# Macaron mLSTM block: early results loaded one group ahead, and a 6 + 2 split of the PSUM banks

## The chip, the core and the metric

The kernel runs on one core of a Trainium2 chip. The metric is the device time of one execution in microseconds (us), as the median of several runs. Engines are named as in the profile: PE (TensorE matmul), PEld (its weight load), DVE (VectorE), ACT (ScalarE), POOL (GpSimd) and SP (SyncE, which here only issues DMAs).

## What is computed

One layer of an encoder on a 1024 x 1024 float32 sequence: a half-step SwiGLU feed-forward (width 2816), a mixing layer (mLSTM and a gating branch), a second half-step feed-forward and a final norm. The change touches only the two feed-forwards and the end:

```
x = x + 0.5 * swiglu(rmsnorm(x, ffn1_norm_g), ffn1_w_in, ffn1_w_out)
...  # mixing layer
x = x + 0.5 * swiglu(rmsnorm(x, ffn2_norm_g), ffn2_w_in, ffn2_w_out)
return rmsnorm(x, final_norm_g)

def swiglu(x, w_in, w_out):
    gate, up = jnp.split(x @ w_in, 2, axis=-1)
    return (jax.nn.silu(gate) * up) @ w_out
```

## The kernel before

Tokens are held transposed, as tiles of 128 features by 512 tokens, in two halves of the sequence (t = 0 and 1). Each matrix is split into a rounded part and a remainder, so one product of four 128-row slices is 12 matmuls of 128 x 512 (three per slice). The feed-forwards use a fast 2 x 2 matrix scheme that needs fewer products: some of them are formed early.

`Ffn.first_products` walks over the 22 groups f of 128 hidden features and forms the products that need only the first half of the tokens. The two results of a group are an accumulated product and the SiLU of it; both are written to DRAM (`self.eb[f][0]` and `self.eb[f][1]`, "eb") through the POOL queue.

`Ffn.run` then walks over the same 22 groups, in blocks of 4, 4, 4, 4, 2 and 4. `Ffn.group(f)` loads the group's weights with four DMAs into two tiles of the pool "raw" (4 buffers; line 284), loads the two early results from DRAM into two tiles "c" (lines 329 and 331), copies the first of them into a PSUM bank x on ACT (line 333), and forms five products onto x, a copy y of it (line 338) and a third bank b (copied out on line 343). Before a product, ACT rounds the weights (line 290) and DVE takes the remainder (line 291) into a tile "fw" (4 buffers); POOL forms sums of the weights ahead of that (lines 303 to 305 and 348). The first product of a group accumulates onto x, so it can't start before the copy of line 333, and that copy can't run before its DMA has landed.

After the first group of every block but the first, the down projection of the block before runs: `down_fast` for blocks of the scheme (four steps of two weight loads, line 386, and seven products; DVE or ACT copies four results per step out into "c" tiles and POOL adds them to DRAM with an accumulating DMA, lines 409 to 424) and `down` for the block of two (16 results, lines 436 and 437). `last` does the final block's down projection: per half t and 128 output features d a product on PE (line 444), the residual add on DVE (line 471) and then the function `final`.

All "c" tiles (early results, copied products, down results) share one pool "t512" of 11 buffers. The PSUM banks, 8 in all, are split into a pool "mm" of 7 and a pool "ml" of 1 during the feed-forwards; `bank("mm")` takes from the one and `psm()` from the other.

In the second feed-forward `final` is `fin2`: it squares and accumulates xt for the norm, transposes xt with PE into a bank (line 1021; up to four 128 x 128 transposes), and DVE multiplies the bank by the norm's weights into the output tile (line 1024). After d = 7 the statistics are finished and the rows are scaled and stored. The second half of the tokens is done in two parts of 256 columns.

What sets the order: the instructions of each engine stand in a queue of their own, which runs strictly in order. The queues are fixed when the kernel is built, by a list scheduler that follows the program text as far as operands are ready, and that hands out the buffers of one pool in the order in which the text asks for them. So a tile can't be written by any instruction ahead of the first write of the tile that the text took from the same pool before it. SP's queue holds the weight loads and the loads of the early results; a weight load waits there until its raw buffer is free, and whatever stands behind it waits too.

Of the kernel before, what the change touches and what calls it, by code (L numbers as in the profile page):

```python
# [19 lines left out]
NF = DFF // P  # L20
# [14 lines left out]
def block_body(ctx, tc, x, ffn1_norm_g, ffn1_w_in, ffn1_w_out, mix_norm_g, w_mix_in, mlstm_conv_w,  # L35
               mlstm_conv_b, mlstm_b_igate, mlstm_b_fgate, mlstm_head_norm_g, sgu_norm_g, sgu_norm_b,
               sgu_w_s, sgu_b_s, w_mix_out, ffn2_norm_g, ffn2_w_in, ffn2_w_out, final_norm_g, out):
    nc = tc.nc
    V, A, PE, G = nc.vector, nc.scalar, nc.tensor, nc.gpsimd
    x = x[0]  # L40
    out = out[0]
# [8 lines left out]
    def open_psum(stack, n, **bufs):  # L50
        for tag, b in bufs.items():
            psum[tag] = stack.enter_context(
                tc.tile_pool(name=f"{tag}{n}", bufs=b, space=bass.MemoryType.PSUM, reuse_waits="tile"))

    def bank(tag):
        return psum[tag].tile([P, NH], F32, tag=tag, name=tag)

    f1 = ExitStack()
# [3 lines left out]
    def open_temps(stack, n, bufs):  # L62
        raws.append(stack.enter_context(tc.tile_pool(name=f"rawp{n}", bufs=3 if n == 2 else 4, reuse_waits="tile")))
        tps.append(stack.enter_context(tc.tile_pool(name=f"tp{n}", bufs=bufs, reuse_waits="tile")))

    open_temps(f1, 1, TMP)
    open_psum(f1, 1, mm=7, ml=1)

    def t512():
        return tps[-1].tile([P, NH], F32, tag="t512", name="t512")  # L70
# [1 line left out]
    def psm():  # L72
        return bank("ml")
# [42 lines left out]
    def pc(nm, i):  # L116
        return par[:, col[nm] + i:col[nm] + i + 1]
# [29 lines left out]
    def spread():  # L147
        if todo:
            todo.pop(0)()
# [115 lines left out]
    def evens(src):  # L265
        return src[:, :, 0, :], src[:, :, 1, :]

    class Ffn:
# [39 lines left out]
        def first_products(self, fs):  # L308
# [9 lines left out]
            for f, a, e in st:  # L318
# [2 lines left out]
                A.activation(out=e[:, 1, :], in_=a, func=AF.Silu)  # L321
                G.dma_start(out=self.eb[f][1], in_=e[:, 1, :])

        def group(self, f):
            r1, r2 = self.raw(f, 0, True), self.raw(f, 1, True)
            a11, a21 = evens(r1)
            a12, a22 = evens(r2)
            p1 = self.c512()
            nc.sync.dma_start(out=p1, in_=self.eb[f][0])
            sg1 = self.c512()  # L330
            nc.sync.dma_start(out=sg1, in_=self.eb[f][1])
            x = bank("mm")
            A.copy(out=x, in_=p1)  # L333
            s1 = self.sums(G, a11, a12, a21, a22, 4)
            w = self.unit(a11)
            self.prod(x, w, self.B["t2"], False, True)
            y = bank("mm")
            A.copy(out=y, in_=x)
            w = self.unit(s1)
            b = bank("mm")  # L340
            self.prod(b, w, self.B["t1"], True, True)
            p5 = self.c512()
            A.copy(out=p5, in_=b)
            w = self.unit(a21)
            self.prod(y, w, self.B["t3"], False, True)
            c22 = self.c512()
            V.tensor_tensor(out=c22, in0=y, in1=p5, op=ALU.add)
            G.tensor_tensor(out=a12, in0=a12, in1=a11, op=ALU.subtract)
            w = self.unit(a12)
            self.prod(x, w, self.B["22"], False, True)  # L350
            V.tensor_tensor(out=p5, in0=x, in1=p5, op=ALU.add)
            A.activation(out=p5, in_=p5, func=AF.Silu)
            w = self.unit(a22)
            self.prod(y, w, self.B["t4"], False, True)
            V.scalar_tensor_tensor(out=sg1, in0=y, scalar=0.5, in1=sg1, op0=ALU.mult, op1=ALU.mult)  # L355
            V.scalar_tensor_tensor(out=c22, in0=c22, scalar=0.5, in1=p5, op0=ALU.mult, op1=ALU.mult)
            u3 = sg1
            if f >= FAST:
                self.hs.append((self.part(self.hp, u3), self.part(bigp, c22)))
            elif f % 2 == 0:  # L360
                self.H["11"].append(self.part(self.hp, u3))
                self.odd = u3, c22
            else:
                h11, h12 = self.odd
                H = self.H
                H["21"].append(self.part(self.hp, u3))
                V.tensor_tensor(out=h11, in0=h12, in1=h11, op=ALU.subtract)
                H["t1"].append(self.part(bigp, h11))
                V.tensor_tensor(out=h12, in0=c22, in1=h12, op=ALU.subtract)
                H["t3"].append(self.part(bigp, h12))  # L370
                V.tensor_tensor(out=h11, in0=c22, in1=h11, op=ALU.subtract)
                H["t2"].append(self.part(bigp, h11))
                V.tensor_tensor(out=u3, in0=u3, in1=h11, op=ALU.subtract)
                H["22"].append(self.part(self.hp, c22))
                H["t4"].append(self.part(bigp, u3))
# [99 lines left out]

        def run(self, src, final, parts, hook):
            pend = None
            for bi, (f0, n) in enumerate(BLOCKS):
                hs = self.hs = []
                H = self.H = {k: [] for k in ("11", "21", "22", "t1", "t2", "t3", "t4")}  # L480
                for f in range(f0, f0 + n):
                    self.group(f)
                    if pend is not None:
                        pend()
                        pend = None
                    spread()
                if f0 < FAST:
                    pend = lambda f0=f0, H=H: self.down_fast(f0, H, src)
                elif bi < len(BLOCKS) - 1:
                    pend = lambda f0=f0, n=n, hs=hs: self.down(f0, n, hs, src)  # L490
                else:
                    self.last(f0, n, hs, src, final, parts, hook)
# [488 lines left out]
        xn2, bcs, st = mix(mx, xnm)  # L981

    with ExitStack() as f2:
        open_psum(f2, 3, mm=7, ml=1)
        open_temps(f2, 3, TMP)
        ffn2 = Ffn(f2, "2", ffn2_w_in[0], ffn2_w_out[0])
        ffn2.B["11"], ffn2.B["21"] = xn2[:4], xn2[4:]

        def get2(j, i, t):
            b = ffn2.c512()  # L990
            d = 4 * j + i
            if t == 0:
                G.dma_start(out=b, in_=xs_[1][d])
                return b
            G.dma_start(out=b, in_=xd[1][t][d])
            V.scalar_tensor_tensor(out=b, in0=b, scalar=pc("g2", d), in1=bcs[t], op0=ALU.mult, op1=ALU.mult)
            return b

        ffn2.first_products((0, 1))
        bcs.append(st.bcast())  # L1000
        for i in range(4):
            ffn2.first_products((2 * i + 2, 2 * i + 3))
            ffn2.operands(i, get2)
        for f in range(10, NF, 2):
            ffn2.first_products((f, f + 1))

        PARTS = (1, 2)
        sts = [[Stats(4 // p) for _ in range(p)] for p in PARTS]
        fgs = []
        ys = []  # L1010

        def fin2(h, d, part, xt):
            n = 4 // PARTS[h]
            if not fgs:
                fgs.append(bigp.tile([P, D], F32, tag="big", name="fg"))
                nc.sync.dma_start(out=fgs[0], in_=final_norm_g.partition_broadcast(P))
            fg = fgs[0]
            sts[h][part].add(xt)
            ps = bank("mm")
            for t in range(n):  # L1020
                PE.transpose(out=ps[:, t * P:(t + 1) * P], in_=xt[:, t * P:(t + 1) * P], identity=ident)  # L1021
            if d % 2 == 0:
                ys.append(bigp.tile([P, n, 2 * P], F32, tag="big", name="y"))
            V.tensor_tensor(out=ys[-1][:, :, (d % 2) * P:(d % 2 + 1) * P],  # L1024
                            in0=ps[:, 0:n * P].rearrange("p (t c) -> p t c", c=P),
                            in1=fg[:, None, d * P:(d + 1) * P].to_broadcast([P, n, P]), op=ALU.mult)
            if d < KT - 1:
                return
            r = sts[h][part].rstd()
            t0 = h * NH + part * n * P  # L1030
            ov = out[t0:t0 + n * P, :].rearrange("(t p) c -> p t c", p=P)
            for i in range(4):
                y = ys.pop(0)
                for t in range(n):
                    if t == n - 1:
                        A.activation(out=y[:, t, :], in_=y[:, t, :], func=AF.Copy, scale=r[:, t:t + 1])  # L1036
                    else:
                        V.tensor_scalar(out=y[:, t, :], in0=y[:, t, :], scalar1=r[:, t:t + 1], scalar2=None,  # L1038
                                        op0=ALU.mult)
                nc.sync.dma_start(out=ov[:, :, i * 2 * P:(i + 1) * 2 * P], in_=y)  # L1040

        ffn2.run(xd[1], fin2, PARTS, lambda t, xs: None)


# [25 lines left out]
```

## Time and profile before

| | before |
|---|---|
| median of 3 runs | 2380.12 us |
| lowest, highest | 2379.06, 2381.86 us |
| the profiled execution, its own time | 2376.19 us |
| its span (first to last instruction) | 2374.4 us |
| mean granted TensorE clock | 0.979 |
| PE busy | 2258.1 us (95% of the span) |
| DVE, ACT, POOL busy | 61%, 47%, 21% |

The first feed-forward's `run` goes from about 143 to 700 us, the mixing layer to about 1640, the second feed-forward's `run` from about 1755 us to the end, of which the last 85 us are `last` with `fin2`. A wait in the profile is the idle time of an engine ahead of an instruction, put down to what released it. The clock is a share of full speed (1.0 is 2.4 GHz, 0.5 is 1.2 GHz).

### The profile page before, as it was taken

How to read it: one execution, taken by the hardware profiler on the slowest of the kernel's cores; microseconds unless marked ns; L12 is line 12 of the kernel's file. 1: busy time of each engine (PE TensorE's matmuls, PEld its weight loads, DVE VectorE, ACT ScalarE, POOL GpSimd, SP SyncE). 2: the span in 40 equal slices, each digit the busy share in tenths (PEclk: the TensorE clock that was granted, in tenths of full speed). 3: DMA queues.
4: the chain of work that ended last, by engine and by line, in shares of the span. 5: the costliest groups of instructions: out<-in, count | busy, mean ns of one | idle time of the engine just before them, and what ended most of it. 6: DMA issues, size and time to landing. Idle time of an engine off the chain costs nothing. (4 is left out here: it accounts for less than half of the span.)

```text
span 2374.4 us, 30679 instructions
## 1 busy us (share of the span) xinstructions
PE 2258.1 (95%) x10979; PEld 1881.8 (79%) x10979; DVE 1453.2 (61%) x2563; ACT 1120.8 (47%) x1924; POOL 496.7 (21%) x557
## 2 busy tenths in 40 slices
PE   7999999999899999999999999999999999999896
PEld 5888787777778988888889878887887787777675
DVE  6647676675366757656656666564647576765355
ACT  5545454444444356444445455453545454544432
POOL 3242433414520000000000000001241524324420
PEclk8999999999999999999999999999999999999999
DMA  8853655637753334233343433325762745646632
GB/s 271 252 179 98 142 117 132 133 89 138 155 186 109 88 85 135 83 89 89 115 129 93 134 113 93 92 83 178 247 190 89 151 108 132 129 120 133 147 110 89
DMA packets 331512, 311.51 MB, mean 131 GB/s; under 512 B 19160, under 2 KB 279896, under 8 KB 331360
## 3 DMA queue, kind: packets, MB, share of 16 engines
q1 hardware_dynamic: 292608, 217.20, 31.1%
q0 software_dynamic: 38752, 92.36, 17.8%
q8 instruction: 86, 1.41, 0.2%
q14 instruction: 66, 0.54, 0.1%
HBM read 223.48 MB, written 86.02 MB: 130 GB/s over the span
## 5 line engine op out<-in xcount | busy, mean ns | idle before, releaser
L297 PE MATMUL mm<-b,fw 128*128 128x512 f32 x2640 | 626.4, 399 | 56.7 <-ACT mm L333 55.7
L297 PEld LDWEIGHTS mm<-b,fw 128*128 128x128 f32 x2640 | 508.1, 193 | 174.6 <-ACT mm L333 64.0
L291 DVE TENSOR_TENSOR fw<-raw,fw 128x512 fp32r<-128x512 f32 (+1 forms) x472 | 316.0, 676 | 396.4 <-ACT fw L290 394.9
L162 PE MATMUL mm<-xn,w 128*128 128x512 f32 x2304 | 546.6, 391 | 0.0
L162 PEld LDWEIGHTS mm<-xn,w 128*128 128x128 f32 x2304 | 427.0, 188 | 82.8
L297 PE MATMUL mm<-h,fw 128*128 128x512 f32 x1344 | 313.6, 393 | 5.8 <-ACT fw L290 3.1
L297 PEld LDWEIGHTS mm<-h,fw 128*128 128x128 f32 x1344 | 248.5, 188 | 69.6 <-ACT fw L290 8.2
L290 ACT CAST fw<-raw 128x512 fp32r<-128x512 f32 (+1 forms) x472 | 247.8, 526 | 101.5 <-PE mm L297 71.6
L138 DVE TENSOR_TENSOR w<-raw,w 128x1024 fp32r<-128x1024 f32 (+3 forms) x160 | 178.6, 1117 | 163.6 <-ACT w L137 163.2
L297 PE MATMUL mm<-xn,fw 128*128 128x512 f32 x1056 | 247.4, 396 | 3.6 <-ACT xn L195 2.1
L297 PEld LDWEIGHTS mm<-xn,fw 128*128 128x128 f32 x1056 | 200.5, 191 | 49.4 <-ACT xn L195 3.7
L137 ACT CAST w<-raw 128x1024 fp32r<-128x1024 f32 (+3 forms) x160 | 153.8, 963 | 178.7 <-PE mm L162 86.2
L176 PE MATMUL mm<-w,xn 128*128 128x256 f32 x1344 | 163.9, 282 | 0.0
L176 PEld LDWEIGHTS mm<-w,xn 128*128 128x128 f32 x1344 | 161.8, 189 | 1.4 <-issue 0.5
L256 POOL DMA_DIRECT2D xs<-t x16 | 8.6, 541 | 642.0 <-DVE t L253 641.3
L195 ACT CAST h<-c 128x512 fp32r<-128x512 f32 x136 | 82.2, 621 | 69.1 <-DVE c L355 26.3
L303 POOL TENSOR_TENSOR s<-raw 128x512 f32<-128x512 f32 x44 | 59.4, 1351 | 205.7 <-DMA raw<-in_ffn_w_in_dram 190.3
L444 PE MATMUL mm<-h,wl 128*128 128x512 f32 (+1 forms) x480 | 97.3, 356 | 0.3 <-DVE h L196 0.2
L196 DVE TENSOR_TENSOR h<-c,h 128x512 fp32r<-128x512 f32 x136 | 91.1, 689 | 5.9 <-ACT h L195 4.8
L409 POOL DMA_DIRECT2D xd<-c x32 | 28.0, 874 | 309.6 <-ACT fw L290 273.0
L444 PEld LDWEIGHTS mm<-h,wl 128*128 128x128 f32 x480 | 78.4, 192 | 12.5 <-DVE h L196 0.7
L162 PE MATMUL po<-mh,w 128*128 128x512 f32 x384 | 87.5, 389 | 0.0
(258 smaller groups left out, 2607.6 us busy)
## 6 DMA issues: line engine op xcount, KB each, us to landing
raw<-in_ffn_w_in_dram SPq DMA_DIRECT2D x264, 256.0 KB, 3.4
raw<-in_w_mix_in_dram SPq DMA_DIRECT2D x96, 512.0 KB, 3.8
xd<-c POOLq DMA_DIRECT2D x160, 256.0 KB, 5.2
eb<-early POOLq DMA_DIRECT2D x88, 256.0 KB, 2.8
c<-eb SPq DMA_DIRECT2D x88, 256.0 KB, 4.3
raw<-in_ffn_w_out_dram SPq DMA_DIRECT2D x72, 256.0 KB, 3.0
raw<-in_w_mix_in_dram SPq DMA_DIRECT2D x32, 384.0 KB, 3.4
xl<-xd POOLq DMA_DIRECT2D x32, 256.0 KB, 4.4
```

The source lines that it names most:

```text
L137: A.copy(out=w[:, 0, 0:n, :], in_=raw[:, 0:n, :])
L138: V.tensor_tensor(out=w[:, 1, 0:n, :], in0=raw[:, 0:n, :], in1=w[:, 0, 0:n, :].bitcast(F32), op=ALU.subtract)
L162: PE.matmul(out=banks[j], lhsT=w[:, a, i, j * P:(j + 1) * P], rhs=act[k][:, b, ts], start=(k == first and pi == 0), stop=(k == last and pi ...
L176: PE.matmul(out=o, lhsT=act[k][:, b, t * P:(t + 1) * P], rhs=w[:, a, i, :], start=(t % 2 == 0 and k == 0 and pi == 0), stop=(t % 2 == 1 an ...
L195: A.copy(out=dst[:, 0, :], in_=src)
L196: V.tensor_tensor(out=dst[:, 1, :], in0=src, in1=dst[:, 0, :].bitcast(F32), op=ALU.subtract)
L290: A.copy(out=w[:, 0], in_=src)
L291: V.tensor_tensor(out=w[:, 1], in0=src, in1=w[:, 0].bitcast(F32), op=ALU.subtract)
L297: PE.matmul(out=bank, lhsT=w[:, x, i, :], rhs=t[:, y, :], start=(start and i == 0 and pi == 0), stop=(stop and i == len(b) - 1 and pi == 2 ...
L303: G.tensor_tensor(out=s1, in0=a21, in1=a22, op=ALU.add)
L409: G.dma_start(out=acc[0][d], in_=c11, accum_op=ALU.add)
L444: PE.matmul(out=o, lhsT=w[:, x, i, :], rhs=hs[i][:, y, ts], start=(i == 0 and pi == 0), stop=(i == n - 1 and pi == 2))
```

## The change

`fetch(f)` takes two tiles from "t512" and issues the loads of the early results of group f on SP. `run` calls it once for group 0; `group(f)` uses the pair that was fetched, and fetches the pair of group f + 1 right after its own weight loads, so in the text ahead of the down projection and of the next group's weights. In both feed-forwards the banks are split 6 + 2 instead of 7 + 1, and the transposes of `fin2` take their bank from the pool of two.

```
-    open_psum(f1, 1, mm=7, ml=1)
+    open_psum(f1, 1, mm=6, ml=2)
...
+        def fetch(self, f):
+            self.ahead = self.c512(), self.c512()
+            for t, src in zip(self.ahead, self.eb[f]):
+                nc.sync.dma_start(out=t, in_=src)
+
         def group(self, f):
             r1, r2 = self.raw(f, 0, True), self.raw(f, 1, True)
             a11, a21 = evens(r1)
             a12, a22 = evens(r2)
-            p1 = self.c512()
-            nc.sync.dma_start(out=p1, in_=self.eb[f][0])
-            sg1 = self.c512()
-            nc.sync.dma_start(out=sg1, in_=self.eb[f][1])
+            p1, sg1 = self.ahead
+            if f + 1 < NF:
+                self.fetch(f + 1)
             x = bank("mm")
             A.copy(out=x, in_=p1)
...
         def run(self, src, final, parts, hook):
             pend = None
+            self.fetch(0)
...
-        open_psum(f2, 3, mm=7, ml=1)
+        open_psum(f2, 3, mm=6, ml=2)
...
             sts[h][part].add(xt)
-            ps = bank("mm")
+            ps = psm()
             for t in range(n):
```

## Rows read from the trace of the kernel before

**Rows 1.** Waits, whole span: who waited for whom, total us, times, longest us.
```profile
ACT mm L333 <- DMA c<-eb: 115.3, 40, 7.8
...
PE mm L297 <- ACT mm L333: 55.7, 18, 9.6
...
PE mm L1021 <- DVE xl L471: 16.8, 23, 3.2
...
SPq L284 <- DVE fw L291: 788.7, 163, 15.5
```
**Rows 2.** Timeline of SP's queue: start, us, operation (weights L284, early results L329).
```profile
257.99 0.44 SPq L329 DMA_DIRECT2D c<-eb  x1
...
261.24 11.91 SPq L284 DMA_DIRECT2D raw<-in_ffn_w_in_dram  x4
273.26 0.45 SPq L329 DMA_DIRECT2D c<-eb  x1
```
**Rows 3.** Timeline of PE, same stretch; in brackets idle before and its releaser.
```profile
265.03 20.93 PE L297 MATMUL mm<-b,fw 128*128 128x512 f32 x84 [3.88 <-ACT mm L333]
...
295.74 14.57 PE L297 MATMUL mm<-b,fw 128*128 128x512 f32 x63 [1.07 <-ACT mm L333]
```
**Rows 4.** Timeline of ACT, same stretch.
```profile
257.43 0.62 ACT L290 CAST fw<-raw 128x512 fp32r<-128x512 f32 x1
...
261.67 0.62 ACT L290 CAST fw<-raw 128x512 fp32r<-128x512 f32 x1
264.39 0.59 ACT L333 COPY mm<-c 128x512 f32<-128x512 f32 x1 [2.09 <-DMA c<-eb]
269.54 0.57 ACT L338 COPY mm<-mm 128x512 f32<-128x512 f32 x1 [4.57 <-PE mm L297]
```
**Rows 5.** Stretches of 8 us, PE: busy (matmuls), granted clock, DMA share, GB/s.
```profile
265.03:273.03 8.00, 8.00 (x28) 0.79 0.65 143
...
2243.99:2251.99 8.00, 8.00 (x24) 0.66 0.59 101
```
**Rows 6.** The same of a stretch behind no long wait, all engines.
```profile
273.03:281.03 8.00, 8.00 (x37) 6.61 (x36) 5.23 (x6) 3.34 (x6) 4.18 (x3) 1.00 0.39 124
```
**Rows 7.** DMA issues: count, size, median us from issue to landing.
```profile
xd<-c POOLq DMA_DIRECT2D x160, 256.0 KB, 5.2
...
c<-eb SPq DMA_DIRECT2D x88, 256.0 KB, 4.3
```
**Rows 8.** Timeline of POOL in the down projection of a two-group block.
```profile
614.60 5.06 POOL L437 DMA_DIRECT2D xd<-c  x5
626.45 1.25 POOL L303 TENSOR_TENSOR s<-raw 128x512 f32<-128x512 f32 x1 [6.78 <-DMA raw<-in_ffn_w_in_dram]
627.65 0.87 POOL L437 DMA_DIRECT2D xd<-c  x1
```
**Rows 9.** Timeline of PE at the end, steps of 512 columns.
```profile
2296.14 0.66 PE L1021 MATMUL mm<-ident,xl 128*128 128x128 f32 x4 [0.78 <-DVE xl L471]
2296.56 2.99 PE L444 MATMUL mm<-h,wl 128*128 128x512 f32 x12
2300.33 0.66 PE L1021 MATMUL mm<-ident,xl 128*128 128x128 f32 x4 [0.79 <-DVE xl L471]
```
**Rows 10.** Timeline of PE at the end, steps of 256 columns.
```profile
2331.62 0.69 PE L1021 MATMUL mm<-ident,xl 128*128 128x128 f32 x2 [3.17 <-DVE xl L471]
...
2335.39 0.44 PE L1021 MATMUL mm<-ident,xl 128*128 128x128 f32 x2 [0.52 <-DVE xl L471]
...
2337.77 0.44 PE L1021 MATMUL mm<-ident,xl 128*128 128x128 f32 x2 [0.52 <-DVE xl L471]
```
**Rows 11.** Three stretches of the end: us, PE, PEld, DVE, ACT, POOL busy (instructions), clock, DMA.
```profile
2289.69:2322.00 32.31, 25.80 (x122) 19.19 (x123) 14.68 (x23) 5.04 (x8) 3.19 (x6) 1.00 0.16 49
2326.58:2335.39 8.81, 5.12 (x29) 4.62 (x29) 6.01 (x23) 2.54 (x6) 0.00 (x0) 0.81 0.64 213
2335.39:2364.75 29.36, 23.00 (x173) 20.48 (x173) 15.68 (x45) 6.81 (x17) 0.00 (x0) 1.00 0.13 44
```

## The prediction
> **What bounds the kernel now.** I read the list of waits first, then timelines around the longest PE waits, then stretches for the clock. PE is busy for 2258.1 of 2374.4 us, so what can be won lies in PE's 116 us of idle time and in time at the lower clock. The waits name one large item: PE sits 55.7 us, in 18 places, behind the copy of line 333, the copy of the early result into x; ACT itself waits 115.3 us, in 40 of 44 groups, for the DMA of that result [rows 1]. The second item is at the end: 16.8 us, 23 times, for the residual add ahead of the transposes [rows 1]. Together they are 72.5 us.
>
> Why the early result is late is seen in SP's queue: it is issued at 257.99, runs 4.3 us in the median [rows 2, 7], and the copy starts at 264.39 [rows 4]. The load isn't slow; it stands behind the weight loads of the following group, and those wait for a raw buffer to come free (788.7 us in all [rows 1]). The same pattern is seen at 261.24 to 273.26: four weight loads first, the early result behind them [rows 2]. In the first group behind a down projection PE pays in full, 3.88 us in the example [rows 3], because PE there is done with the down projection when the load has just been issued.
>
> Ten of the 18 places are of that kind: eight behind `down_fast` (3.9 to 4.4 us, the first in [rows 3]; 33.5 us) and two behind `down` (7.0 and 9.6 us, the longest in [rows 1]; 16.5 us). The other eight are of 0.25 to 1.8 us, one of them 1.07 [rows 3], and make 5.7 us.
>
> **The early results, one group ahead.** The change removes no DMA and adds none: 88 loads of 256 KB stay [rows 7]. It moves each pair up by one group on SP's queue. Buffers of "t512" are handed out in text order, and the pair of group f + 1 now stands in the text where the pair of f stood. So it takes the place in the queue that the pair of f has now. The load that is issued at 273.26 [rows 2] would then serve the group that starts at 295.74 [rows 3] and not the one before: 22 us of lead against a flight of 4.3. Behind a down projection the lead grows further, since the pair is asked for ahead of the whole down projection. All 18 waits should go: 55.7 us.
>
> What is late next? In the example the weights of the coming group were rounded from 257.43 on, the fourth rounding at 261.67 [rows 4], ahead of the copy at 264.39. PE went on without another gap for 84 matmuls, 20.9 us [rows 3]. So x alone was missing there, and I put nothing in the place of the waits behind `down_fast`.
>
> The clock comes back too. In the 8 us from the end of the ten long waits the granted clock averages 0.62 to 0.81 (first and last of the ten [rows 5]), against 1.00 in a stretch behind no long wait [rows 6]; the matmuls in 8 us fall from 37 to 23 to 29. The two levels are 1.2 and 2.4 GHz, and PE had stood idle just before. The ten clocks (0.79, 0.69, 0.71, 0.79, 0.76, 0.62, 0.81, 0.79, 0.68, 0.66) lack 2.70 of ten full ones, times 8 us: 21.6 us. No short wait (up to 1.8 us) is followed by such a fall. This part stands or falls with the ten long waits: 0 if they stay, 21.6 if they go.
>
> What the prefetch costs: two more of the 11 buffers are held, so a down projection cycles through fewer. A result's buffer is busy from its copy until its accumulating DMA has landed, 5.2 us in the median from issue [rows 7]. In `down_fast` four results a step leave time for that. In `down` 16 results come within some 20 us, and POOL stops issuing for 6.8 us because a sum of weights ahead of the DMAs waits for its load [rows 8]; the six results behind it keep their buffers until after 627.65 + 5.2. The third product's copy of the next group (line 347, DVE) may then wait for one of these buffers; behind DVE stand the weight remainders, and behind them PE. Nothing before shows this wait. Its bounds are 0 (another buffer is free) and the length of POOL's stop, 6.8, in each of two places, with a fall of the clock of 2.2 (21.6 / 10) behind it: 0 to 18 us. I take 3, since x is now copied early and frees a buffer just there.
>
> Moving the pair past the weights pushes weight loads back by its issue time, 0.45 and 0.4 us [rows 2]; the weights are loaded a group ahead, so it is hidden. If that cover were gone it would cost 44 x 0.85 = 37 us.
>
> **Six banks.** A group needs x, y and b; with x of the next group copied early, and its y and b behind it, six. A step of `down_fast` needs four and the next step's first two, again six. No wait of PE for a bank of "mm" is among the waits that I read, and an early x adds one bank. I cost it at 0, with bounds of 0 and 44 group starts at a short wait like the 0.25 to 1.8 us above, at its mean (5.7 / 8 = 0.7): 31 us. I am nearer to 0, as a bank taken six allocations back is at least a step old. The Trainium skill (TensorE: Matmul & The Clock Gate, "A second HAM failure mode: psum-queue depth-cycling") says that cycling through banks can give PE short idles so often that its clock falls back. Here 23 short idles at the end, 0.52 to 0.79 us each, ran at a granted clock of 1.00 [rows 9 to 11], so the trace doesn't bear it out; it is the fourth rival below.
>
> **Transposes in the pool of two.** Before, line 1021 and the products of line 444 take banks from one pool, so the next product can't begin before the transposes of the last one have: PE runs product, wait for the add, transposes, product. With a pool of their own the next product needs not wait, and the transposes come in the middle or after it. A step of 512 columns is 4.19 us (2296.14 to 2300.33), of which 0.78 is the wait [rows 9]. Counted by starts it could shrink by up to 1.0 (the wait, and a drain that the next product would cover); seven of the eight steps gain: 5.5 to 7 us. A step of 256 columns is 2.38, with a wait of 0.52 [rows 10]; 14 gain 0.52 to 0.74: 7 to 10 us. The 3.17 us wait at 2331.62 [rows 10], while DVE scales the first half's rows, can be filled with one product, and with it goes part of a slow clock (0.81 over 8.81 us [rows 11]): 1.5 to 4 us. PE is busy 25.8 of 32.3 and 23.0 of 29.4 us there, DVE 14.7 and 15.7 [rows 11], so neither DVE nor two banks, which DVE empties within a step, should become the bound. Sum 14 to 21, bounds 0 and 21; I take 15, since the transposes may be put so early into the product that a part of the wait stays.
>
> **The sum.** 55.7 + 21.6 - 3 + 15 = 89.3 us. The profiled execution took 2376.2 us with a span of 2374.4, so it would come to 2286.9; it lies 3.9 under the median of 2380.1, which gives 2290.8. I predict 2290.
>
> **Rivals.** First, the end gains nothing (the order there stays product, add, transposes, or the two banks make it so): 2290 + 15 = 2305. For it: I can't see the new order. Against: nothing but the shared pool ties them now.
>
> Second, the x wait is replaced by another. The next weights, the POOL sums or the buffers of "t512" are late in most first groups behind a down projection, and half of 77.3 us is lost: 2290 + 39 = 2329. For it: POOL waits on loads in [rows 8]. Against: the weights are there in [rows 4].
>
> Third, slower: the down projections stall on "c" buffers. The two held tiles make the copy of a result wait for an accumulating DMA; ACT and DVE stand in order, so the weights behind the copy are late and PE stops in each of the ten down projections. It decides from 9 us for each, where it has eaten the 89 us; with POOL's stop of 6.8, a DMA's 5.2 and the clock's 2.2 at all ten (142 us) the time is 2380 + 142 - 89 = 2433. For it: [rows 8]. Against: there it hits six results of 16, in two of the ten places.
>
> Fourth, the clock falls with six banks: if the end ran at half clock, its 25.8 + 23.0 us of PE work [rows 11] would take as long again: 2290 + 49 = 2339.
>
> Fifth, the change doesn't do what it says: SP still issues the pair late, because the weight loads ahead of it wait longer, and only the end gains: 2380 - 15 = 2365. Against: the place in the queue exists already [rows 2].
>
> **How the numbers follow.** Chances: forecast (2275 to 2303) 0.70, end without gain 0.08, another wait 0.10, slower 0.05, clock 0.02, no prefetch 0.05. The range reaches down to all bounds won (2380.1 - 55.7 - 21.6 - 21 and some pipeline fill at 18 starts, 2278, less 3) and up to half of the second rival: 2275 to 2318; it leaves out some 0.18. A difference under 0.2% (5 us) can't be told from none here. Faster 0.93; same 0.02 (the slower rival half come true); slower 0.05.
>
> **What would show it.** Right: no wait of PE or ACT on line 333's DMA; the loads of eb on SP a group ahead of use; no stretch at half clock in the two `run` loops; at the end products of line 444 start before the transposes of the step before, with steps near 3.3 and 1.8 us. Wrong: new waits of PE behind line 291, of ACT or DVE on a DMA of "xd<-c", or of PE on the eviction of line 1024. Most of the sum is one reading, that x alone is late at the ten places; if the profile shows PE still idle there, the forecast fails by up to 77 us.

## The result and the profile after

The changed kernel took 2283.28 us in the median (2275.98 to 2284.43), against 2380.99 for the kernel before in the same session: a ratio of 0.958, 95% interval 0.956 to 0.961, a gain of 98 us in the medians. The forecast was 2290 with a range of 2275 to 2318. The profiled execution took 2283.09 us with a span of 2281.3; before it was 2376.19 with 2374.4.

The stretches of the two kernels, side by side, say where the time went. Columns: stretch, its length, then busy time of PE, PEld, DVE, ACT and POOL (with instructions), granted clock, DMA share, GB/s. The stretches are: first `run` loop, what lies between the loops, second `run` loop, `last` up to the statistics of the first half, rest. The kernel before:

```profile
152.59:673.94 521.35, 490.52 (x2090) 396.08 (x2089) 327.80 (x517) 250.05 (x486) 189.23 (x173) 0.97 0.57 129
673.94:1764.33 1090.39, 1078.05 (x5839) 928.32 (x5838) 663.25 (x1239) 517.38 (x744) 59.15 (x103) 0.99 0.40 121
1764.33:2287.61 523.28, 491.65 (x2090) 396.86 (x2089) 328.56 (x517) 250.41 (x486) 189.38 (x174) 0.97 0.56 130
2287.61:2323.30 35.69, 29.13 (x140) 21.67 (x140) 17.24 (x26) 5.72 (x10) 4.04 (x8) 1.00 0.16 53
2323.30:2374.40 51.10, 31.93 (x229) 28.38 (x228) 26.06 (x84) 13.58 (x32) 0.21 (x1) 0.91 0.28 93
```

The changed kernel:

```profile
151.16:633.73 482.57, 478.53 (x2090) 389.84 (x2089) 343.38 (x517) 251.06 (x486) 192.47 (x173) 1.00 0.60 139
633.73:1723.76 1090.03, 1078.30 (x5839) 928.47 (x5838) 663.00 (x1239) 517.17 (x744) 59.54 (x104) 0.99 0.40 121
1723.76:2215.78 492.02, 481.25 (x2090) 391.64 (x2089) 349.42 (x517) 251.34 (x486) 195.05 (x173) 0.99 0.60 137
2215.78:2243.93 28.15, 28.10 (x144) 22.12 (x143) 16.79 (x26) 6.57 (x11) 3.55 (x7) 1.00 0.19 65
2243.93:2281.30 37.37, 28.16 (x225) 26.69 (x225) 25.23 (x85) 12.45 (x32) 0.72 (x2) 0.90 0.39 127
```

Read the second column downwards: the loops lose 38.8 and 31.3 us, the end 7.5 and 13.7 (21.3 together), the middle, which the change hardly touches, 0.4. With 1.4 ahead of the loops that is the 93.1 us between the two profiled executions; the medians lie 98 apart. PE's busy time in the loops falls too, by 12.0 and 10.4 us at the same 2090 matmuls, because the clock goes from 0.97 to 1.00 and 0.99.

The waits (who waited for whom, total us, times, longest) show what is gone and what is left. Line numbers moved: the copy of the early result is line 337 now, the copy x to y 342, the copy of b 347, the copy of the third product 351, the final transposes 1026, the load of the early results 327.

```profile
ACT mm L337 <- DMA c<-eb: 7.9, 3, 4.0
...
PE mm L297 <- ACT mm L342: 4.9, 6, 1.6
PE mm L297 <- DVE c L351: 4.7, 1, 4.7
...
PE ml L1026 <- DVE xl L475: 0.5, 1, 0.5
...
SPq L284 <- DVE fw L291: 736.5, 163, 12.1
...
SPq L327 <- DMA xd<-c: 15.5, 9, 7.4
```

[rows 1] had 115.3 us of ACT for the early result, 55.7 of PE behind its copy, 16.8 of PE ahead of the transposes. The second is gone altogether, the others are 7.9 and 0.5. The 4.7 us behind line 351 are new, and so are the 15.5 us in which SP's loads of the early results wait for a buffer. The weights' own waits for buffers are 736.5 us where they were 788.7. (Line 351 is DVE's sum of y and the copied b into a "c" tile; it is called the third product's copy here, as in the prediction.)

SP's queue, at the place of [rows 2]:

```profile
259.30 5.46 SPq L284 DMA_DIRECT2D raw<-in_ffn_w_in_dram  x4
264.87 3.30 SPq L327 DMA_DIRECT2D c<-eb  x2
271.54 11.89 SPq L284 DMA_DIRECT2D raw<-in_ffn_w_in_dram  x4
283.48 0.97 SPq L327 DMA_DIRECT2D c<-eb  x2
```

The pattern is the one of [rows 2], four weight loads and a pair behind them. Only the pair now belongs to a later group: the group that PE starts at 259.05 had its copy of line 337 at 254.44, and the next copy runs at 263.16, ahead of both issues shown. PE at that place has no gap where [rows 3] had 3.88 us:

```profile
259.05 43.15 PE L297 MATMUL mm<-b,fw 128*128 128x512 f32 x187
```

And the end, steps of 512 and of 256 columns, against [rows 9, 10]:

```profile
2229.26 0.66 PE L1026 MATMUL ml<-ident,xl 128*128 128x128 f32 x4
2229.68 3.01 PE L448 MATMUL mm<-h,wl 128*128 128x512 f32 x12
2232.55 0.66 PE L1026 MATMUL ml<-ident,xl 128*128 128x128 f32 x4
...
2249.03 4.31 PE L448 MATMUL mm<-h,wl 128*128 128x256 f32 x34
...
2266.22 0.44 PE L1026 MATMUL ml<-ident,xl 128*128 128x128 f32 x2
2266.42 1.68 PE L448 MATMUL mm<-h,wl 128*128 128x256 f32 x12
2268.02 0.44 PE L1026 MATMUL ml<-ident,xl 128*128 128x128 f32 x2
```

A step of 512 columns takes 3.29 us (2229.26 to 2232.55) where it took 4.19, one of 256 takes 1.80 where it took 2.38, and none of these transposes waits. At 2249.03, where DVE scales the first half's rows, 34 matmuls run in one piece: nearly three products ahead.

### The profile page after: what moved, and what is told of

It is laid out like the page before. It is cut to its first block, busy times and chain, and to the rows that moved or that the text cites. A ratio compares the mean times of both kernels' runs of the same rounds, so it can differ in the third digit from the quotient of the medians.

```text
span 2281.3 us, 30658 instructions
## 1 busy us (share of the span) xinstructions
PE 2230.2 (98%) x10979; PEld 1868.4 (82%) x10979; DVE 1488.2 (65%) x2563; ACT 1123.0 (49%) x1924; POOL 506.3 (22%) x557
## 5 line engine op out<-in xcount | busy, mean ns | idle before, releaser
L297 PE MATMUL mm<-b,fw 128*128 128x512 f32 x2640 | 605.6, 391 | 9.6 <-ACT mm L342 4.9
L297 PEld LDWEIGHTS mm<-b,fw 128*128 128x128 f32 x2640 | 496.6, 188 | 116.7 <-ACT mm L342 7.4
L291 DVE TENSOR_TENSOR fw<-raw,fw 128x512 fp32r<-128x512 f32 (+1 forms) x472 | 328.7, 703 | 297.4 <-ACT fw L290 295.7
L196 DVE TENSOR_TENSOR h<-c,h 128x512 fp32r<-128x512 f32 x136 | 101.8, 776 | 10.0 <-ACT h L195 8.9
```

The costliest lines, as they stand in the source:

```text
L196: V.tensor_tensor(out=dst[:, 1, :], in0=src, in1=dst[:, 0, :].bitcast(F32), op=ALU.subtract)
L291: V.tensor_tensor(out=w[:, 1], in0=src, in1=w[:, 0].bitcast(F32), op=ALU.subtract)
L297: PE.matmul(out=bank, lhsT=w[:, x, i, :], rhs=t[:, y, :], start=(start and i == 0 and pi == 0), stop=(stop and i == len(b) - 1 and pi == 2 ...
```

## The experiments

### Each part alone

The fetch without the banks and without the end's new pool:

```
             p1, sg1 = self.ahead
             if f + 1 < NF:
                 self.fetch(f + 1)
...
     open_psum(f1, 1, mm=7, ml=1)
...
             ps = bank("mm")
```

> The kernel before with the fetch one group ahead alone; banks stay 7 + 1 and the final transposes stay in the pool of products. My theory: the ten long and eight short waits for the early result go, and the ten stretches at half clock behind them: 55.7 + 21.6 - 3 = 74 us, so 2381 - 74 = 2307, within 2302 to 2312. Rival one, the split into 6 + 2 banks helps the fetch (or the fetch needs it): the gain is well under 74, say 40, 2341. Rival two, what the change gained beyond the forecast (97.7 against 89.3) comes from here, by short waits in all groups: 83 us, 2298.

Measured: 2300.8 us against 2378.6, ratio 0.968 (0.966 to 0.971), 75 us gained (70 to 81) where 74 were expected. Its two loops:

```profile
151.36:635.56 484.20, 479.61 (x2090) 389.51 (x2089) 343.63 (x517) 251.03 (x486) 191.95 (x173) 1.00 0.60 138
...
1724.63:2209.79 485.16, 478.28 (x2090) 389.83 (x2089) 344.33 (x517) 251.30 (x486) 192.72 (x173) 1.00 0.60 139
```

They lose 37.2 and 38.1 us against the kernel before, at a clock of 1.00, and the end stays at 86.8 us. So the fetch doesn't need the new split of the banks, and it isn't the part that gave more than forecast.

The end's part without the fetch:

```
-    open_psum(f1, 1, mm=7, ml=1)
+    open_psum(f1, 1, mm=6, ml=2)
...
-            ps = bank("mm")
+            ps = psm()
```

> The kernel before with the banks 6 + 2 and the final transposes in the pool of two, without the fetch. My theory: the end gains 15 us (bounds 0 to 21): 2366; the list of waits keeps 55.7 us behind the copy of line 333. With the run of the fetch alone it should add up to the whole change. Rival: what the change gained beyond the forecast lies in the end, 23 us: 2358. Second rival: the gain of the end belongs to the fetch as well, and here it is below 10: over 2371.

Measured: 2356.6 us, ratio 0.991 (0.989 to 0.993), 21 us gained (16 to 26). The wait behind line 333 is still there (64.0 us, 20 times); `last` and what follows take 65.6 us, as in the changed kernel (65.5). With the 75 of the fetch this makes 96 of the 98 us: the parts add up. The first rival of that expectation holds: the end gave 21 and not 15.

The split of the banks alone (the same diff without its last two lines):

> The kernel before with the banks 6 + 2 alone; the transposes still take their bank from the pool of products. My theory: six banks cost nothing, 2381 within 5, and the end is as before, steps of 4.2 and 2.4 us. Rival: each of 44 group starts waits some 0.7 us more for a bank, up to 31 us slower, 2412. Second rival, the clock falls when PE cycles through fewer banks: the stretches at the end go below a clock of 1.00 and the time is up by up to 49 us.

Measured: 2378.8 us, ratio 1.000 (0.9985 to 1.0018). Six banks for products cost nothing, within some 4 us, and bring nothing by themselves: the transposes still wait 0.79 us in each step of 512 columns, as in [rows 9].

### Is the low clock PE's idle time?

```
             w = self.unit(a11)
+            fill = {5: 17, 9: 17, 13: 17, 17: 17, 19: 30}.get(f, 0)
+            if fill:
+                z = psm()
+                for i in range(fill):
+                    PE.matmul(out=z, lhsT=w[:, 0, 0, :], rhs=self.B["t2"][0][:, 0, :], start=(i == 0),
+                              stop=(i == fill - 1), skip_group_check=True)
             self.prod(x, w, self.B["t2"], False, True)
```

> The kernel before, with matmuls of no use put ahead of the first product of the ten groups behind a down projection: 17 in the eight behind the fast form, 30 in the two behind the plain one, all of 128 x 512 into the spare bank. They have their operands while the early result is still missing, so PE works where it waited (17 x 0.22 = 3.7 us of 3.9 to 4.4; 30 x 0.22 = 6.5 of 7.0 and 9.6). The early results come as late as before. My theory: the half-clock stretches follow from PE's idle time and most go, while the path keeps the wait: a gain of 15 to 21.6 us, 2360 to 2366. Rival: the clock falls for another reason (the DMA load, or the group's start itself) and stays low: the matmuls gain nothing, 2381, or cost time, up to 10 us.

Measured: 2357.5 us, ratio 0.991 (0.989 to 0.994), 21 us gained (15 to 27) with 196 matmuls more. The early results were as late as before, and PE was busy in the meantime. PE's first row in a group behind a down projection:

```profile
259.66 4.01 PE L340 MATMUL ml<-b,fw 128*128 128x512 f32 x17
```

Then the waits:

```profile
ACT mm L333 <- DMA c<-eb: 120.1, 40, 5.5
PE mm L297 <- ACT mm L333: 9.2, 17, 1.3
```

And the two loops:

```profile
150.99:663.57 512.58, 503.52 (x2188) 407.34 (x2187) 329.21 (x517) 249.88 (x486) 189.87 (x173) 1.00 0.58 131
...
1756.82:2265.28 508.46, 502.37 (x2188) 407.67 (x2187) 326.60 (x517) 249.91 (x486) 190.24 (x173) 1.00 0.58 134
```

ACT's wait is unchanged (120.1 us), PE's is down to 9.2, and the clock of both loops is 1.00. The DMA share is nearly that of before (0.58 against 0.57 and 0.56). So the half clock followed from PE standing idle there, and the 21 us that the run gave back agree with the 21.6 that I read off the ten stretches of [rows 5].

### What made the early result late

I argued that it was the order in which buffers of one pool are handed out, not the place of the load in the text. So the load stays where it was, with buffers of its own:

```
-TMP = 11
+TMP = 9
...
+            self.ep = pool("fe", 2)
...
-            p1 = self.c512()
+            p1 = self.ep.tile([P, NH], F32, tag="e", name="c")
             nc.sync.dma_start(out=p1, in_=self.eb[f][0])
```

> The kernel before, with no fetch: the first early result of a group takes its tile from a pool of its own of 2 buffers, and the shared pool is cut from 11 to 9. The loads stand in the text where they stood, behind the weight loads of their group. My theory: what made the load late was that its buffer was handed out in text order behind other tiles; with a pool of its own the load of group f + 2 can go as soon as group f has been copied, and the waits and the half-clock stretches go as in the run with the fetch: 2379 - 74 = 2305, within 2298 to 2312. Rival one, the text's place behind the weight loads keeps it late: 2379. Rival two, 9 buffers are too few for the down projections: over 2312, with waits on accumulating DMAs.

Measured: 2304.7 us, ratio 0.969 (0.966 to 0.972), as the fetch alone. No wait of ACT for an early result is left, and SP issues the two loads of a group apart, the first one (line 330) before the weights that stand ahead of it in the text:

```profile
265.12 0.34 SPq L330 DMA_DIRECT2D c<-eb  x1
265.55 1.10 SPq L285 DMA_DIRECT2D raw<-in_ffn_w_in_dram  x2
266.82 1.06 SPq L332 DMA_DIRECT2D c<-eb  x1
```

Two buffers of its own do what the change does with a new order in the text.

### Does the end need the second bank?

```
-    open_psum(f1, 1, mm=6, ml=2)
+    open_psum(f1, 1, mm=7, ml=1)
```

in both feed-forwards of the changed kernel.

> The changed kernel with the banks back at 7 + 1, so that the final transposes have one bank of their own. My theory: it is the separate pool that frees the products, and one bank is emptied within a step, so the steps at the end stay at 3.3 and 1.8 us and the loss is 0 to 3 us: 2283 to 2286. Rival one, the second bank is needed, since transposes of a step wait for the eviction of the step before: steps of 3.7 and 2.1 us, 8 x 0.4 + 16 x 0.3 = 8 us slower, 2291. Rival two, nothing of the gain is left: 2304.

Measured: 2279.1 us, ratio to before 0.958 (0.956 to 0.961), that of the changed kernel. Steps of 512 columns take 3.29 us here as well. What the end gained came from the separate pool; the 6 + 2 split isn't needed.

### The new stop, and what buffers cost

The 4.7 us behind line 351 stand in the group behind `down`, in the second feed-forward. Five kernels, and the changed kernel once more, were run to see what it hangs on. First, two buffers fewer (`TMP = 9` in the changed kernel):

> The changed kernel with 9 buffers in the shared pool in place of 11. My theory: the third product's copy that waited once for an accumulating DMA behind a two-group down projection (4.7 us of PE and 3.4 of clock in the changed kernel's profile) is for want of a buffer; with two fewer both such places stop PE for up to POOL's 6.8 us or more, and the clock falls behind them: 10 to 40 us slower than the changed kernel, 2293 to 2323, and the waits on accumulating DMAs rise from 15.5 us on SP and 1.6 on ACT. Rival one, the buffers aren't what it waits for: 2283 within 5. Rival two, the slower rival of the prediction decides here: all ten down projections stop, 2380 and above.

Measured: 2289.6 us, ratio 0.963 (0.960 to 0.966), 6 us over the changed kernel by the medians, 11 by the ratios (whose intervals overlap), less than or at the lower end of what I expected. It waits in other places: ACT for accumulating DMAs (9.8 us at line 440 and 3.6 at line 427, against 1.6 in all), and PE 4.8 us behind the copy of line 337 in the two groups behind `down`. PE doesn't stop behind line 351 at all. So two buffers are worth some 6 to 11 us in the slower rival's direction, far from deciding, and my theory of a stop for want of a buffer didn't hold.

Next, one buffer less held by the fetch:

```
-            self.ahead = self.c512(), self.c512()
-            for t, src in zip(self.ahead, self.eb[f]):
-                nc.sync.dma_start(out=t, in_=src)
+            self.ahead = self.c512()
+            nc.sync.dma_start(out=self.ahead, in_=self.eb[f][0])
...
+            sg1 = self.c512()
+            nc.sync.dma_start(out=sg1, in_=self.eb[f][1])
```

> The changed kernel, but only the first early result is fetched a group ahead; the second (used at the end of the group) is loaded in its own group, behind that group's weights. One buffer fewer is held over the down projections. My theory: the copy of the third product finds a buffer behind the two-group down projection, and the 4.7 us wait of PE and the 3.4 us of clock that the changed kernel's profile shows go: 2275 to 2280. Rival one, that stop is chance of one execution and its mean cost is nothing: 2283 within 3. Rival two, the second early result comes too late in its own group, as the first did before: 10 us or more slower, 2293.

Measured: 2283.6 us, ratio 0.960 (0.957 to 0.963): no change. My theory fell: PE stopped behind the same copy, now 3.9 us in the first feed-forward and 1.2 in the second.

The changed kernel once more, beside the three runs that follow:

> The changed kernel once more, as the measure for the runs beside it: a ratio to before of 0.956 to 0.960. It also shows whether the stop behind the two-group down projection (4.7 us of PE and 3.4 of clock, in the second feed-forward alone) comes at the same place in another execution: my theory says that it moves or varies, since it hangs on when the weights land; the rival, that it is fixed by the order of the queues, says 4 us or more at the same place again.

Measured: 2284.8 us, ratio 0.960 (0.958 to 0.962). The stop varies: 3.4 us in the first feed-forward and 2.3 in the second, where the first profile had none and 4.7.

Then the pair asked for behind the copy that stopped:

```
-            if f + 1 < NF:
+            if f + 1 < NF and f != 19:
                 self.fetch(f + 1)
...
+            if f == 19:
+                self.fetch(f + 1)
             G.tensor_tensor(out=a12, in0=a12, in1=a11, op=ALU.subtract)
```

> The changed kernel, but in group 19 (the group behind the two-group down projection) the pair of group 20 is asked for after the third product's copy and not before it. The copy that stopped PE for 4.7 us then gets a buffer that comes free two results earlier, and SP issues that group's last weights ahead of the pair. Theory: the stop is for want of a buffer at just that point, so it goes, with the half-clock stretch behind it: 3 to 8 us faster than the changed kernel, 2275 to 2280. Rival one: the stop's mean cost is small, as the run with one tile fetched suggests: within 3 us of the changed kernel. Rival two: the pair of group 20 is now late, and a wait for the early result of some 4 us returns at two places: 2283 to 2295.

Measured: 2278.4 us, ratio 0.958 (0.956 to 0.960), 6 us under the 2284.8 of the changed kernel beside it, which is about what can be told apart. No wait of PE behind line 351 is in its profile. With the banks at 7 + 1 as well:

> The same as the run with the pair of group 20 behind the third copy, and the banks back at 7 + 1. The run of the changed kernel at 7 + 1 gave 2279. Theory: the eighth bank is of no use in either place, so the time is that of the other run within 3 us. Rival: a seventh bank for products takes away some of the short waits for the copy of line 342 (4.9 us in all): 2 to 5 us faster than the other run.

Measured: 2281.5 us, ratio 0.958 (0.956 to 0.961): the same within some 3 us, as the theory said.

Last, one buffer more, taken from the sums (`TMP = 12`, `pool("fs", 1)`):

> The changed kernel with 12 buffers in the shared pool; the memory for it is taken from the pool of weight sums, which goes from 2 buffers to 1. Theory: one more buffer takes the stop behind the two-group down projection away, 3 to 8 us faster than the changed kernel, 2275 to 2280, if one buffer of sums is enough. Rival one: the stop isn't decided by one buffer: 2283 within 3. Rival two: the sums of a group now wait until the second unit of the group before has been rounded, POOL falls behind, and PE waits for weights of line 348's group: 44 x 0.5 = 20 us or more slower, 2303.

Measured: 2299.3 us, ratio 0.966 (0.964 to 0.968), 14.5 us slower than the changed kernel beside it. With one buffer more for copies the stop grew to 5.0 and 6.4 us. The run also took a buffer of sums away, so alone it doesn't settle the matter; but with nine buffers there was no stop behind that copy, and with twelve it is longer: fewer "c" buffers didn't bring it on and one more didn't take it away. The second rival is nearest: POOL's sums wait 37.6 us for remainders of weights, against 15.9 and 6.1 in the two profiles of the changed kernel, though the stops of PE are again behind `down` and not in all 44 groups.

The profile of the changed kernel shows the chain. PE's fourth product of group 19 ends at 2178.4 (2183.09 less the 4.69 of idle time); the fifth accumulates onto y, which the copy of line 351 has to read first. In the rows below (start, length, engine, line; idle before in brackets) SP issues the last two weight loads of group 20 at 2159.52; POOL's sum of them can start only at 2173.32; ACT rounds the formed weight at 2178.95, DVE takes its remainder at 2179.61, and only then comes the copy of group 19 (line 351), for which PE waits:

```profile
2159.52 0.94 SPq L284 DMA_DIRECT2D raw<-in_ffn_w_in_dram  x2
...
2158.51 5.11 POOL L441 DMA_DIRECT2D xd<-c  x5
2173.32 1.28 POOL L303 TENSOR_TENSOR s<-raw 128x512 f32<-128x512 f32 x1 [9.71 <-DMA raw<-in_ffn_w_in_dram]
...
2178.95 0.62 ACT L290 CAST fw<-raw 128x512 fp32r<-128x512 f32 x1 [2.38 <-POOL raw L305]
...
2179.01 2.05 POOL L352 TENSOR_TENSOR raw<-raw 128x512 f32<-128x512 f32 x1
...
2181.93 3.20 POOL L303 TENSOR_TENSOR s<-raw 128x512 f32<-128x512 f32 x1
...
2179.61 2.73 DVE L291 TENSOR_TENSOR fw<-raw,fw 128x512 fp32r<-128x512 f32 x1 [7.44 <-ACT fw L290]
2182.26 0.68 DVE L351 TENSOR_TENSOR c<-mm,c 128x512 f32<-128x512 f32 x1
...
2183.09 2.47 PE L297 MATMUL mm<-b,fw 128*128 128x512 f32 x5 [4.69 <-DVE c L351]
```

The weights of group 20 stand ahead of the copy of group 19 in DVE's queue, and they are late because their load took some 13 us. In the first feed-forward of the same execution the same pair of loads, issued at 584.42, let POOL start its sum at 591.30, 6 to 7 us later, and PE didn't stop. In the run that asks for the pair behind the copy, POOL waited 5.4 and 3.6 us for that load, against 9.0 and 7.1 in the two stops of the changed kernel beside it. In the second feed-forward, the sum of the changed kernel and then that of the other run:

```profile
2177.86 1.29 POOL L303 TENSOR_TENSOR s<-raw 128x512 f32<-128x512 f32 x1 [7.07 <-DMA raw<-in_ffn_w_in_dram]
...
2169.57 1.28 POOL L303 TENSOR_TENSOR s<-raw 128x512 f32<-128x512 f32 x1 [3.60 <-DMA raw<-in_ffn_w_in_dram]
```

The stop doesn't need the fetch: the run with a pool of its own, which has none, stops for 3.8 us behind the same copy, its line 348:

```profile
PE mm L298 <- DVE c L348: 4.2, 2, 3.8
```

And the kernel before has the late sum of POOL at this place, 6.78 us behind a weight load [rows 8], with no stop of PE behind its line 347: while that load was on its way PE stood waiting for x (6.99 us, up to 631.07).

Why the load is fast in one execution and slow in the next stays open, and with it how much of that run's 6 us is its own doing.

## Why the prediction was right, step by step

**The reading of the bottleneck** held. The early result was late because its buffer came late (the run with a pool of its own), and x alone was missing in the first groups behind `down_fast`: nothing took the place of those eight waits. The prediction saw the load behind the weights in SP's queue; the run with a pool of its own shows that the order of the buffers had put it there.

**The x waits** were sized at 55.7 us and are gone to the last one (0 of 18 left). A small item came in their place: 4.9 us behind the copy of line 342, in six waits of up to 1.6 us.

**The clock**, 21.6 us: right in mechanism and in size; the run with filled waits gives 21 (15 to 27). In the changed kernel's first profile no short wait in the loops is followed by a fall of the clock either, but my statement that waits of up to 1.8 us never are is too wide: in the run that asks for the pair behind the copy, one of 1.76 us was (a clock of 0.79 over the next 8 us).

**The new wait behind `down`**, taken at 3 with bounds of 0 and 18: the place was right and the cause was not. I named the copy of the third product waiting for a buffer behind POOL's accumulating DMAs. It is that copy which PE waits for, but what holds it is the next group's weights ahead of it in DVE's queue, and those wait for a load. The prediction had that load in hand: POOL's stop in [rows 8] is the same late sum, which I let act through the buffers and not through DVE's order. In the changed kernel's first profile it cost 4.7 us and 2.6 of clock (0.67 over the next 8 us; PE's second loop is 7 us longer than with the fetch alone), in its second profile 3.4 and 2.3 us without the clock, in the fetch's own profile 1.0.

```profile
2183.09:2191.09 8.00, 8.00 (x24) 6.38 (x25) 7.32 (x8) 2.49 (x4) 6.90 (x5) 0.67 0.98 219
```

(The 3.4 us of clock in the expectations of three runs came from a stretch that began 1.5 us before PE went on.) The 3 stands within that, by luck as far as the cause goes. The queue that I didn't think through is SP's: in the changed kernel a pair can wait 7.4 us for its own buffer (15.5 us in 9 waits) with weight loads behind it.

**Six banks** at 0: right (1.000, within some 4 us), so was the view that PE's short idles at the end don't lower its clock. Of the 23 idles that the prediction calls short, 22 are; the other is the one of 3.17 us, in the stretch at 0.81 [rows 11]. The end now has no idle between steps but one of 0.52 us at the last, and a clock of 1.00 from 2215.78 to 2271.59, so the rule on cycling through banks (the Trainium skill, TensorE: Matmul & The Clock Gate, "A second HAM failure mode: psum-queue depth-cycling") was not seen at work on either side of this change.

**The end** was the mis-sized term: 15 taken, 21 measured, the upper bound. The steps came out as counted: 7 x 0.90 = 6.3 (5.5 to 7 given) and 14 x 0.58 = 8.1 (7 to 10 given). What is left of 21.3, some 7 us, lies mostly where DVE scales the rows of the first half: the two steps there took 8.81 us [rows 11], and two of 1.80 are 5.2 less. I had allowed 1.5 to 4 there, for one product run ahead in the 3.17 us wait. With a pool of their own for the transposes the whole pool "mm" is free for products, and nearly three of them ran ahead there, so PE didn't stop and the clock from 2243.93 to 2258.00 stayed at 1.00 (0.81 over 8.81 us in [rows 11]). The haircut for transposes put into the middle of a product was not needed either.

**The sum** was thus 8 us short: 6 at the end. The other 2 can't be put to a term: for the 74 us of the loops the two profiles with the fetch show 70.0 (with the stop of 4.7 us) and 75.3.

**The rivals.** The end without gain is refuted by the run of the end's part; the wait in place of the x wait is real at two of ten places, and costs 0 to 7 us and not 39; the slower rival was tried with 9 buffers and came to 6 to 11 us; the clock with six banks and the fetch that doesn't fetch are refuted by the runs of each part.

## What to carry to other kernels

When a load is late, look first at what its buffer is shared with: in a pool whose buffers go out in text order, the load waits for everything asked for ahead of it. Here a small pool of its own was worth the same as an earlier request (2304.7 and 2300.8 us). When a long wait goes, look for a shorter one that it covered: the late sum of POOL was in the profile before. Price a stall at the engine's idle time plus the slow clock behind it, and read that second part from the stretch that follows: here it was another 40% of the first (21.6 of 55.7 us). When a use is moved out of a shared pool, count what the engine can then run ahead, not only the wait that is removed.

## What the runs showed that was not expected

A 256 KB weight load took some 13 us where the median of the whole execution is 3.4. It was issued among accumulating DMAs of POOL; between 2155 and 2180 us the queue of POOL's DMAs (software_dynamic) took 62% of the DMA engines' time, and the six weight loads took 7.3 us in the median. The share by queue and the issues (count, size, median us to landing) of that stretch:

```profile
q0 software_dynamic: 1318, 2.39, 62.2%
q1 hardware_dynamic: 4508, 2.62, 35.8%
...
raw<-in_ffn_w_in_dram SPq DMA_DIRECT2D x6, 256.0 KB, 7.3
```

The issues of the whole execution:

```profile
raw<-in_ffn_w_in_dram SPq DMA_DIRECT2D x264, 256.0 KB, 3.4
...
xd<-c POOLq DMA_DIRECT2D x160, 256.0 KB, 5.3
```

DVE's remainder at 2179.61 took 2.73 us, against 0.69 for the same operation at 2169.79 and 2171.47, where POOL stood idle. POOL's subtraction (2179.01 to 2181.06) had started first and ran beside it for 1.45 us; the copy of line 351, one of whose operands is a PSUM bank, took its usual 0.68 beside the next sum of POOL (2181.93). The Trainium skill (SBUF — State Buffer, "SBUF: two separate sides") says that DVE and GpSimd take turns on a shared port when a DVE operation has two inputs in SBUF and the GpSimd operation reads SBUF. The rows agree with it in direction: of the excess of 2.04 us it would account for the 1.45 beside the subtraction, and the other 0.6 stays unexplained. DVE's busy time in the two loops rose by 36 us with the change, at the same 517 operations in each; how much of that is this sharing was not measured.
